# Half-array matmul pairs in the recurrence scores and the windowed attention of a two-layer encoder trunk

## The chip, the core and the metric

The kernel runs on one core of a Trainium2 chip. The metric is the device time of one execution in microseconds (us). The engines are named as in the profile: PE is TensorE (PEld its weight loads), DVE is VectorE, ACT is ScalarE, POOL is GpSimd, SP is SyncE. A core has 128 partitions; TensorE multiplies a stationary operand (up to 128 rows by 128 columns) with a moving one and writes to PSUM, which is used here as 8 banks of 512 FP32 columns.

## What is computed

Two sequences of 512 and 256 tokens, 1024 wide, go through two layers with shared weights. Each layer is a feed-forward block, a token mixer and another feed-forward block, each behind an RMS norm. The mixer of the first layer is a gated linear recurrence in both directions (8 heads of 128), that of the second a windowed attention (16 query heads in 4 groups, 64 wide, +-128 tokens, a sink logit for each head). Cut to the two mixers:

```python
# recurrence, per head and direction: S_t = diag(f_t) S_{t-1} + k_t v_t^T,  o_t = S_t^T q_t
A = einsum('bthk,btshk,bshk->bhts', qf, exp(rel), kf)   # within a chunk
o = einsum('bthk,bhkv->bthv', qf * exp(b), S) + einsum('bhts,bshv->bthv', A, vf)

# windowed attention, per block of 128 queries against up to three blocks of 128 keys
s = where(mask, einsum('bnqhgd,bnkhd->bnhgqk', q, k) * d ** -0.5, -inf)
m = maximum(max(s), sink)
p = exp(s - m); denom = sum(p) + exp(sink - m)
o = einsum('bnhgqk,bnkhd->bnqhgd', p / denom, v)
```

## The kernel before

The 768 tokens are handled together as 6 blocks of 128 (`NBLK`), 4 of the long sequence and 2 of the short. Most matrix products are made of three matmuls on a rounded FP32 type (`F32R`): an operand is split into a high half (a cast by ScalarE) and a low half (a subtraction by VectorE) by `split`, and high x high, high x low and low x high are accumulated (`mm3`, L258 to L260). The feed-forward blocks, whose matmuls are at L418 and L482, aren't touched by the change. Plain FP32 operands are used in the recurrence itself.

*Recurrence.* `hgrn` works through the 8 heads. `hgrn_scan` does one head: within each block of 128 tokens, the 128 x 128 matrix `A` of scores (rows are keys, columns are queries, both directions together) is built in 7 levels of doubling size `J` = 1 to 64, plus the diagonal. At each level ScalarE gathers the keys into `kop` (L699), `scan_scores` multiplies each block's keys with that block's queries (L674: six FP32 matmuls of 128 x 128 x 128 into two banks, 4 blocks in one and 2 in the other), and `put` writes the entries that belong to this level into `A` on VectorE: a plain copy at level 0 (L688), a masked copy (`copy_predicated`, L693) at the others. Then VectorE multiplies the decays into the queries (L716) and keys (L720) for the next level. The generator yields after each level, and `weave` puts pieces of the next head's projections (matmuls at L258 to L260) between two levels. Each engine gets its instructions in the order in which the program issues them.

*Attention.* `swa` projects keys and values (`put_kv`) and queries (`put_q`), applies the rotary embedding (`rotate`), and works through 24 units, one for each of 4 groups and 6 query blocks, each with 4 heads. A unit has stages: `query` splits its queries into halves that lie side by side, `turn` transposes them (L913), so that 64 partitions hold the high half and 64 the low half; `scores` multiplies them with the transposed keys, where the high half of the keys stands on both sets of 64 partitions, and then the low half (two matmuls a head, L1109 and L1110, so all four products); a fused VectorE instruction adds the band and takes the minimum (L1112); `exps`, `sink` and `denominator` make probabilities; `probs` transposes them (L1147) and splits them into halves; `values` multiplies them with the values, whose halves lie side by side as 128 stationary columns (L1159, L1160, 512 moving columns each); `finish` adds the two halves (L1165, L1170). `split_out` splits the outputs once more for the output projection `out_proj`. `pipeline` sorts the stages of all units by a hand-written step and rank, with pieces of the query projection and of the output projection as fillers.

Of the kernel before, what the change touches and what calls it, by code (L numbers as in the profile page):

```python
# [27 lines left out]
KV = 4  # L28
# [19 lines left out]
class Trunk:  # L48
# [621 lines left out]
    def scan_scores(self, pss, lhs, rhs):  # L670
        nc = self.nc
        for b in range(NBLK):
            s, i = (0, b) if b < 4 else (1, b - 4)
            nc.tensor.matmul(pss[s][:, i * P : (i + 1) * P], lhs(b), rhs(b), start=True, stop=True)  # L674

    def hgrn_scan(self, hd, v):
# [19 lines left out]
        for l in range(LEVELS):  # L696
            c, J = T >> l, 1 << l
            kv = bass.AP(k.tensor, k.offset, [list(k.ap[0]), [2 * J, c // 2], [T + J, 2], [1, J]])
            nc.scalar.copy(kop.rearrange("p (b g j) -> p b g j", g=2, j=J), kv)  # L699

            def rhs(b):
                return bass.AP(
                    q.tensor, q.offset + b * P, [list(q.ap[0]), [2 * J, P // (2 * J)], [T + J, 2], [1, J]]
                )

            pss = [self.ps(n) for _, n in SEQS]
            self.scan_scores(pss, lambda b: blk(kop, b), rhs)
            put(l, pss)
            if l == 0:
                pss = [self.ps(n) for _, n in SEQS]  # L710
                self.scan_scores(pss, lambda b: blk(kd, b), lambda b: blk(qs, b))
                put(LEVELS, pss)
# [12 lines left out]
            tot, base = totals, nbase  # L725
            yield
# [76 lines left out]
    def hgrn(self, lb_row, gn_row, next_row):  # L803
# [92 lines left out]
        self.drain(self.out_proj("hg_o", 0, uT, None))  # L896
        self.drain(self.out_proj("hg_o", 1, uT, next_row))

    def rotate(self, ps, heads, pos, t):
        nc = self.nc  # L900
        v = lambda t: t.rearrange("p (h d) -> p h d", d=HD)
        x, tv = v(ps), v(t)
# [12 lines left out]
    def swa(self, next_row):  # L915
# [3 lines left out]
        kT = [self.big([P, 2, T], F32R) for _ in range(KV)]  # L919
        vv = [self.big([P, 3, KV, P], F32R) for _ in range(2)]  # L920

        def put_kv(s, b, ps):
            off, n = SEQS[s]
            gb = off // P + b
            st = self.big([P, KV, 2, P], F32R)
            kh, kl = st[:, :, 0, :], st[:, :, 1, :]
            k = self.tmp(256)
            self.rotate(ps[:, :256], KV, b, k)
# [3 lines left out]
            src = ps[:, 256:].rearrange("p (g d) -> p g d", d=HD)  # L932
            v = vv[gb // 3][:, gb % 3]
            nc.scalar.copy(v[:, :, :HD], src)
            nc.vector.tensor_sub(v[:, :, HD:], src, v[:, :, :HD].bitcast(F32))

            def rest():
                for g in range(KV):
                    pt = self.ps(256)
                    for i in range(2):  # L940
                        self.transpose_r(pt[:, i * P : (i + 1) * P], st[:, g, i, :])
                    nc.scalar.copy(kT[g][:, :, gb * P : (gb + 1) * P], pt.rearrange("p (a b) -> p a b", a=2))
# [6 lines left out]
        def put_q(half):  # L949
            def f(s, b, ps):  # L950
# [4 lines left out]
                self.rotate(ps, 512 // HD, b, t)  # L955
# [6 lines left out]
        tiles = [None] * NC  # L962
        of = {}

        def units(gs):
            def alloc(g):
                if g not in of:
                    of[g] = self.big([P, 2, T])
# [8 lines left out]
        def split_out(gs):  # L977
            for g in gs:
                for i in range(2):
                    for s, (off, n) in enumerate(SEQS):  # L980
                        if s == 0:
                            tiles[2 * g + i] = self.big([P, 2, T], F32R)
                        t = tiles[2 * g + i]
                        hi, lo = t[:, 0, off : off + n], t[:, 1, off : off + n]
                        src = of[g][:, i, off : off + n]
                        nc.scalar.copy(hi, src)
                        nc.vector.tensor_sub(lo, src, hi.bitcast(F32))  # L987

        q = itertools.chain(self.proj_tok("q0", put_q(0)), self.proj_tok("q1", put_q(1)))
        wo = self.out_proj("sw_o", 0, tiles, None)  # L990
# [6 lines left out]
        extra.append((60, lambda: split_out((0,))))  # L997
        extra.append((65, lambda: split_out((1,))))
        extra += [(66 + i * 5 / 4, piece(wo)) for i in range(24)]
        extra.append((84, lambda: split_out((2,))))  # L1000
        self.pipeline(list(units(range(KV))), extra)
        split_out((3,))
        self.drain(wo)
        self.drain(self.out_proj("sw_o", 1, tiles, next_row))

    def out_proj(self, tag, half, act, next_row):
        for c in range(2):
            for b in range(NBLK):
                ps = self.ps()
                sl = slice(b * P, (b + 1) * P)  # L1010
                for i in range(4):
                    key = (tag, half, c, i // 2)
                    wh, wl = self.take(key)
                    t = act[half * 4 + i]
                    self.mm3(ps, (t[:, 0, sl], t[:, 1, sl]), (wh[:, i % 2, :], wl[:, i % 2, :]), i == 0, i == 3)
# [32 lines left out]
    def pipeline(self, units, extra):  # L1048
# [5 lines left out]
        for i, u in enumerate(units):  # L1054
            t = 4 * i
            at(t - (3 if i else 5), 5, u.query)
            at(t - 2, 3.5, u.turn)
            for h in range(GQ):
                at(t + h // 2, 0, lambda u=u, h=h: u.scores(h))
# [15 lines left out]
class Unit:  # L1075
    def __init__(self, k, s, b, g, q, kT, vv, of):
        self.k, self.s, self.b, self.g, self.q = k, s, b, g, q
        self.kT, self.vv, self.of = kT[g], vv, of
# [7 lines left out]
        self.split = {}  # L1086

    def query(self):
        k = self.k
        q = self.q().rearrange("p (h d) -> p h d", d=HD)  # L1090
        self.st = k.big([P, GQ, P], F32R)
        k.split(q, self.st[:, :, :HD], self.st[:, :, HD:])

    def turn(self):
        k, nc = self.k, self.k.nc
        pt = k.ps()
        for i in range(GQ):
            k.transpose_r(pt[:, i * P : (i + 1) * P], self.st[:, i, :])
        self.qT = k.tmp(512, F32R)
        nc.scalar.copy(self.qT, pt)  # L1100

    def scores(self, i):
        k, nc = self.k, self.k.nc
        if i == 0:
            self.sc = k.big([P, GQ, 3 * P])
            self.nm, self.den, self.sk = (k.stat(GQ) for _ in range(3))
        ps = k.ps(self.nk)
        qi = self.qT[:, i * P : (i + 1) * P]
        nc.tensor.matmul(ps, qi, self.kT[:, 0, self.keys], start=True, stop=False)  # L1109
        nc.tensor.matmul(ps, qi, self.kT[:, 1, self.keys], start=False, stop=True)  # L1110
        h = self.g * GQ + i
        nc.vector.tensor_tensor_reduce(  # L1112
            self.sc[:, i, : self.nk],
            ps,
            self.band,
            -(HD**-0.5),
            k.nsinks[:, h : h + 1],
            ALU.add,
            ALU.min,
            self.nm[:, i : i + 1],  # L1120
        )
# [21 lines left out]
    def probs(self, j):  # L1143
        k = self.k
        pt = k.ps()
        for i in range(GQ):
            k.nc.tensor.transpose(pt[:, i * P : (i + 1) * P], self.sc[:, i, j * P : (j + 1) * P], k.ident)  # L1147
        hi, lo = k.tmp(512, F32R), k.tmp(512, F32R)
        k.split(pt, hi, lo)
        self.split[j] = (hi, lo)  # L1150

    def values(self, j):
        k, nc = self.k, self.k.nc
        if j == 0:
            self.po = k.ps()
        gb = self.off // P + self.k0 + j
        v = self.vv[gb // 3][:, gb % 3, self.g, :]
        hi, lo = self.split[j]
        nc.tensor.matmul(self.po, v, hi, start=(j == 0), stop=False)  # L1159
        nc.tensor.matmul(self.po, v, lo, start=False, stop=(j == self.nkb - 1))  # L1160

    def finish(self):
        k, nc = self.k, self.k.nc
        low = k.tmp(512)
        nc.scalar.copy(low[:HD, :], self.po[HD:, :])  # L1165
        of = self.of()
        lo = self.off + self.b * P
        for par in range(2):
            r = lambda t: t.rearrange("p (c a q) -> p c a q", a=2, q=P)[:, :, par, :]
            nc.vector.tensor_add(of[par * HD : (par + 1) * HD, :, lo : lo + P], r(self.po[:HD, :]), r(low[:HD, :]))  # L1170
# [114 lines left out]
```

## Time and profile before

| | |
|---|---|
| median of 3 runs | 2833.57 us (2833.03 to 3576.69) |
| the profiled execution | 2833.56 us, of which the profile's span is 2831.8 us |
| PE, PEld, DVE, ACT, POOL busy | 2790.5, 2559.2, 2203.1, 1320.2, 307.3 us |
| recurrence scans on TensorE | 580.90 to about 958 us of the span |
| attention units | about 2105 to 2300 us of the span |

A row of a group of instructions gives the line, the engine and operation, output <- inputs by the program's names (for a matmul the moving operand, then the stationary one), the shape, how often, busy time in us and the mean duration of one in ns, and then how long the engine was idle just before them and who ended that. A matmul row also says how many rows and columns of the array are active (128*128). In a timeline a row begins with start and length in us. A row of a table of windows gives the window, its length, the busy time and count of each engine, the granted TensorE clock as a share of full speed, the share of DMA and GB/s. A row of waits names who waited for whom, the total in us, the number of times and the longest.

### The profile page before, as it was taken

The page shows a single profiled execution, that of the slowest core. Times are in us where ns is not written, and L with a number is a line of the kernel's source. Part 1 is how long each engine was busy: PE and PEld are TensorE (multiplying, and loading weights), DVE is VectorE, ACT ScalarE, POOL GpSimd, SP SyncE. Part 2 cuts the span into 40 slices and gives each one's busy share as a digit, 9 for nine tenths or more (in the row PEclk, how much of TensorE's full clock was granted, in tenths as well). Part 3 has the DMA queues.
Part 4 walks back from the last instruction along what each step waited for, and adds up shares of the span by engine and source line. Part 5 has one row for each costly group of instructions (what it writes and reads, how often), then busy time and mean ns, then how long its engine had stood idle before and what let it go on. Part 6 is the DMA issues. An engine that isn't in the chain of part 4 may idle for free.

```text
span 2831.8 us, 40534 instructions
## 1 busy us (share of the span) xinstructions
PE 2790.5 (99%) x15225; PEld 2559.2 (90%) x15225; DVE 2203.1 (78%) x3846; ACT 1320.2 (47%) x2453; POOL 307.3 (11%) x306
## 2 busy tenths in 40 slices
PE   8999999999999999999999999999999899999998
PEld 8999999889899889999999999999887779999998
DVE  7888788477577558888878887887859978878877
ACT  7444443434344336444444643444457756434443
POOL 1111111000000001111111111111100001111110
PEclk9999999999999999999999999999999999999999
DMA  5554554311111133555454355554412113555543
GB/s 157 133 126 119 124 140 122 112 45 38 43 40 38 60 97 75 140 131 122 120 121 119 82 142 129 123 122 112 144 60 75 40 43 82 142 132 121 122 113 108
DMA packets 330100, 291.37 MB, mean 103 GB/s; under 512 B 11608, under 2 KB 257840, under 8 KB 329904
## 3 DMA queue, kind: packets, MB, share of 16 engines
q1 hardware_dynamic: 294064, 212.43, 25.6%
q0 software_dynamic: 31680, 62.93, 13.3%
q10 hardware_dynamic: 4160, 13.42, 1.3%
q8 instruction: 119, 1.95, 0.3%
q14 instruction: 77, 0.63, 0.1%
HBM read 216.39 MB, written 9.44 MB: 80 GB/s over the span
## 4 chain that ended last, share of the span: by engine, by line
PE 91%; DVE 6%; ACT 2%; issue 1%; DMA 0%; DVEq 0%; ACTq 0%; SPq 0%
PE ps L418 38%; PE ps L482 20%; PE ps L259 8%; PE ps L258 8%; PE ps L260 8%; PE ps L674 3%; PE ps L768 1%; DVE w L200 1%; DVE big L264 1%; PE ps L320 1%; PE ps L1147 1%; PE ps L744 1%; DVE w L167 0%; PE ps L1109 0%; DVE big L1112 0%
## 5 line engine op out<-in xcount | busy, mean ns | idle before, releaser
L418 PE MATMUL ps<-big,w 128*128 128x384 f32 x6720 | 1173.8, 335 | 1.5 <-ACT tA L435 1.4
L418 PEld LDWEIGHTS ps<-big,w 128*128 128x128 f32 x6720 | 1165.2, 188 | 8.4 <-ACT tA L435 6.4
L199 ACT CAST w<-wr 128x512 fp32r<-128x512 f32 x600 | 416.1, 707 | 689.2 <-DVE wr L213 342.8
L200 DVE TENSOR_TENSOR w<-wr,w 128x512 fp32r<-128x512 f32 (+1 forms) x520 | 447.8, 865 | 185.8 <-ACT w L199 174.8
L482 PE MATMUL ps<-w,big 128*128 128x512 f32 x2520 | 576.6, 390 | 0.7 <-DVE x L504 0.6
L482 PEld LDWEIGHTS ps<-w,big 128*128 128x128 f32 x2520 | 472.1, 188 | 100.1 <-ACT big L263 1.5
L504 DVE SCALAR_TENSOR_TENSOR x<-ps,x 128x512 f32<-128x512 f32 x468 | 304.3, 683 | 10.8 <-PE ps L260 10.0
L141 POOL DMA_DIRECT2D s<-wr x120 | 105.3, 877 | 1821.2 <-DMA wr<-in_ffn_w_dram 649.6
L258 PE MATMUL ps<-w,big 128*128 128x512 f32 x624 | 248.9, 399 | 0.3
L260 PE MATMUL ps<-w,big 128*128 128x512 f32 x624 | 244.9, 393 | 1.8 <-DVE big L327 1.0
L259 PE MATMUL ps<-w,big 128*128 128x512 f32 x624 | 244.2, 391 | 0.0
L258 PE MATMUL ps<-big,w 128*128 128x384 f32 (+2 forms) x640 | 221.4, 347 | 2.1 <-ACT big L263 2.0
L263 ACT CAST big<-tA 128x384 fp32r<-128x384 f32 x296 | 148.0, 513 | 151.5 <-DVE tA L450 70.3
L259 PE MATMUL ps<-big,w 128*128 128x384 f32 (+2 forms) x640 | 217.5, 340 | 0.7 <-DVE big L264 0.5
L260 PE MATMUL ps<-big,w 128*128 128x384 f32 (+2 forms) x640 | 216.3, 338 | 0.0
L264 DVE TENSOR_TENSOR big<-tA,big 128x384 fp32r<-128x384 f32 x296 | 180.3, 620 | 12.9 <-ACT big L263 12.0
L167 DVE TENSOR_TENSOR w<-wr,w 128x1024 fp32r<-128x1024 f32 x92 | 111.6, 1220 | 79.3 <-ACT w L166 73.6
L166 ACT CAST w<-wr 128x1024 fp32r<-128x1024 f32 x92 | 96.6, 1052 | 118.8 <-PE ps L259 100.2
L260 PEld LDWEIGHTS ps<-w,big 128*128 128x128 f32 x624 | 117.1, 188 | 28.0 <-DVE big L987 1.7
L200 POOL TENSOR_TENSOR w<-wr,w 128x512 fp32r<-128x512 f32 x80 | 123.8, 1547 | 166.9 <-ACT w L199 146.9
L259 PEld LDWEIGHTS ps<-w,big 128*128 128x128 f32 x624 | 117.4, 188 | 22.3
L258 PEld LDWEIGHTS ps<-w,big 128*128 128x128 f32 x624 | 117.3, 188 | 22.2 <-issue 0.3
(169 smaller groups left out, 3213.3 us busy)
## 6 DMA issues: line engine op xcount, KB each, us to landing
wr<-in_ffn_w_dram SPq DMA_DIRECT2D x264, 512.0 KB, 3.9
s<-in_ffn_w_dram SPq DMA_DIRECT2D x120, 256.0 KB, 3.3
s<-wr POOLq DMA_DIRECT2D x120, 256.0 KB, 4.4
wr<-wr POOLq DMA_DIRECT2D x80, 256.0 KB, 3.7
wr<-in_hg_w_in_dram SPq DMA_DIRECT2D x40, 512.0 KB, 3.8
wr<-wr POOLq DMA_DIRECT2D x20, 512.0 KB, 4.6
spill<-x ACTq DMA_DIRECT2D x12, 512.0 KB, 2.8
x<-spill ACTq DMA_DIRECT2D x12, 512.0 KB, 3.3
```

The lines of the kernel that those rows point to most:

```text
L141: self.nc.gpsimd.dma_start(out, src, accum_op=ALU.add)
L167: self.nc.vector.tensor_sub(lo, raw, hi.bitcast(F32))
L199: nc.scalar.copy(h, src)
L200: low = (eng or nc.vector).tensor_sub(l, src, h.bitcast(F32)).ins
L258: nc.tensor.matmul(out, a[0], b[0], start=first, stop=False)
L259: nc.tensor.matmul(out, a[0], b[1], start=False, stop=False)
L260: nc.tensor.matmul(out, a[1], b[0], start=False, stop=last)
L263: self.nc.scalar.copy(hi, src)
L264: self.nc.vector.tensor_sub(lo, src, hi.bitcast(F32))
L418: self.nc.tensor.matmul(ps, a[x], b[y], start=first and k == 0 and i == 0, stop=k == 3 and i == 2, skip_group_check=True,)
L482: nc.tensor.matmul(ps, a[x], w[y], start=name == chain and kp == 0 and q == 0, stop=kp == 1 and q == 2, skip_group_check=True,)
L504: self.nc.vector.scalar_tensor_tensor(x, ps, c, x, ALU.mult, ALU.add)
```

## The change

In the recurrence only half of each block of scores is computed at a level. A call of 128 keys and 128 queries becomes two, each with 64 stationary columns (64 keys) and 64 moving columns (64 queries): the first half of the keys writes partitions 0 to 63, the second half 64 to 127, of one bank for all six blocks. At levels 0 to 5 and on the diagonal, keys meet the queries of their own half; at level 6 (`J` = 64) those of the other half. `put` then writes two pieces of 64 partitions; level 6 is now a plain copy.

In the attention, keys and queries are transposed first and split afterwards. Keys stand twice, on partitions 0 to 63 and 64 to 127 (a copy by POOL before the transpose). The queries of two heads stand one above the other; `scores` handles two heads at a time, one on the upper and one on the lower 64 rows of the array, with three matmuls each, alternating between the heads, into two banks. `probs` no longer splits: the probabilities stay FP32, and `values` uses the FP32 values as 64 stationary columns, with two heads' probabilities (256 columns) into partitions 0 to 63 and those of the other two into 64 to 127. `finish` splits the result straight into the halves that `out_proj` needs, and `split_out`, `query` and the adds are gone. In `pipeline`, `turn` takes the step that `query` had.

```diff
-    def scan_scores(self, pss, lhs, rhs):
+    def scan_scores(self, lhs, rhs):
+        ps = self.ps(NBLK * 64)
         for b in range(NBLK):
-            s, i = (0, b) if b < 4 else (1, b - 4)
-            nc.tensor.matmul(pss[s][:, i * P : (i + 1) * P], lhs(b), rhs(b), start=True, stop=True)
+            for par in range(2):
+                rows = slice(par * 64, (par + 1) * 64)
+                self.nc.tensor.matmul(ps[rows, b * 64 : (b + 1) * 64], lhs(b)[:, rows], rhs(b, par), start=True, stop=True)
+        return ps
...
-        def put(level, pss):
-            for s, (off, n) in enumerate(SEQS):
-                dst = A[:, off : off + n]
-                if level == 0:
-                    nc.vector.tensor_copy(dst, pss[s])
+        def put(level, ps):
+            for par in range(2):
+                rows = slice(par * 64, (par + 1) * 64)
+                c = 1 - par if level == LEVELS - 1 else par
+                dst = A.rearrange("p (b c j) -> p b c j", c=2, j=64)[rows, :, c, :]
+                src = ps[rows, :].rearrange("p (b j) -> p b j", j=64)
+                if level in (0, LEVELS - 1):
+                    nc.vector.tensor_copy(dst, src)
                     continue
-                nb = n // P
-                m = self.masks[:, level, :].unsqueeze(1).to_broadcast([P, nb, P])
-                r = lambda t: t.rearrange("p (b j) -> p b j", b=nb)
-                nc.vector.copy_predicated(r(dst), m, r(pss[s]))
+                m = self.masks[rows, level, c * 64 : (c + 1) * 64].unsqueeze(1).to_broadcast([64, NBLK, 64])
+                nc.vector.copy_predicated(dst, m, src)
...
-            def rhs(b):
-                return bass.AP(
-                    q.tensor, q.offset + b * P, [list(q.ap[0]), [2 * J, P // (2 * J)], [T + J, 2], [1, J]]
-                )
+            def rhs(b, par):
+                part = list(q.ap[0])
+                if J == 64:
+                    return bass.AP(q.tensor, q.offset + b * P + (0 if par else T + J), [part, [1, J]])
+                at = q.offset + b * P + par * 64
+                return bass.AP(q.tensor, at, [part, [2 * J, 64 // (2 * J)], [T + J, 2], [1, J]])
...
         def put_kv(s, b, ps):
...
-            self.split(k.rearrange("p (h d) -> p h d", d=HD), kh[:, :, :HD], kl[:, :, :HD])
-            nc.scalar.copy(kh[:, :, HD:], kh[:, :, :HD].bitcast(F32))
-            nc.scalar.copy(kl[:, :, HD:], kl[:, :, :HD].bitcast(F32))
...
+            self.rotate(ps[:, :256], KV, b, st[:, :, 0, :])
+            nc.gpsimd.tensor_copy(st[:, :, 1, :], st[:, :, 0, :])
+            nc.scalar.copy(vv[:, gb], ps[:, 256:].rearrange("p (g d) -> p g d", d=HD))
...
             def rest():
+                pt = self.ps()
                 for g in range(KV):
...
+                    nc.tensor.transpose(pt[:, g * P : (g + 1) * P], col, self.ident)
+                for i in range(KV // 2):
+                    src = pt[:, i * 2 * P : (i + 1) * 2 * P].rearrange("p (g t) -> p g t", g=2)
+                    self.split(src, *(t[:, :, gb * P : (gb + 1) * P] for t in kT[i]))
...
+    def turn(self):
...
+        for i in range(2):
+            k.nc.tensor.transpose(pt[:, i * P : (i + 1) * P], q[:, i * P : (i + 1) * P], k.ident)
+        t = k.tmp(512, F32R)
+        self.qT = t[:, :256], t[:, 256:]
+        k.split(pt, *self.qT)
...
-        nc.tensor.matmul(ps, qi, self.kT[:, 0, self.keys], start=True, stop=False)
-        nc.tensor.matmul(ps, qi, self.kT[:, 1, self.keys], start=False, stop=True)
...
+        pss = [k.ps(self.nk) for _ in range(2)]
+        for j, (x, y) in enumerate(((0, 0), (0, 1), (1, 0))):
+            for par in range(2):
+                rows = slice(par * HD, (par + 1) * HD)
+                q = self.qT[x][rows, p * P : (p + 1) * P]
+                nc.tensor.matmul(pss[par], q, self.kT[y][rows, self.keys], start=j == 0, stop=j == 2)
...
-        hi, lo = k.tmp(512, F32R), k.tmp(512, F32R)
-        k.split(pt, hi, lo)
-        self.split[j] = (hi, lo)
...
+        self.pT[j] = k.tmp(512)
+        k.nc.scalar.copy(self.pT[j], pt)
...
-        nc.tensor.matmul(self.po, v, hi, start=(j == 0), stop=False)
-        nc.tensor.matmul(self.po, v, lo, start=False, stop=(j == self.nkb - 1))
+        for par in range(2):
+            nc.tensor.matmul(
+                self.po[par * HD : (par + 1) * HD, :],
+                v,
+                self.pT[j][:, par * 256 : (par + 1) * 256],
...
     def finish(self):
...
+        self.k.split(self.po.rearrange("p (c q) -> p c q", c=2), *(t[:, :, lo : lo + P] for t in self.of()))
```

TensorE's instructions in the first head's scan, levels 0 and diagonal and what follows: before (a call of FP32 stands in one row; x4 means four in a row; `big_4938` are the queries, `big_5151` holds `kop` and `A`):

```order
L260 MATMUL ps_5125<-big_4597,w_4929 128x512
L674 MATMUL ps_5154<-big_4938,big_5151 128x128 x4
L674 MATMUL ps_5155<-big_4938,big_5151 128x128 x2
L674 MATMUL ps_5164<-big_4936 128x128 x4
L674 MATMUL ps_5165<-big_4936 128x128 x2
L258 MATMUL ps_5178<-big_4590,w_4928 128x256
```

and in the changed kernel, at the same place:

```order
L260 MATMUL ps_5125<-big_4597,w_4929 128x512
L675 MATMUL ps_5154<-big_4938,big_5151 64x64 x12
L675 MATMUL ps_5169<-big_4936 64x64 x12
L258 MATMUL ps_5188<-big_4590,w_4928 128x256
L259 MATMUL ps_5188<-big_4590,w_4928 128x256
```

Six calls of 128 x 128 into two banks became twelve of 64 x 64 into one; the matmuls around them stayed.

VectorE at the same place, before (copies into `A` at L688 and L693, decays at L716, L720 and L722, a weight split at L167):

```order
L688 COPY big_5151<-ps_5154 128x512
L688 COPY big_5151<-ps_5155 128x256
L716 TENSOR_TENSOR big_4938<-big_4938,big_4937 128x2x384
L693 COPY_PREDICATED big_5151<-big_4691,ps_5164 128x512
L693 COPY_PREDICATED big_5151<-big_4691,ps_5165 128x256
L720 TENSOR_TENSOR big_4939<-big_4939,big_5152 128x192x2 x2
L167 TENSOR_TENSOR w_5204<-wr_4932,w_5203 128x1024
```

and in the changed kernel (the same operations stand at L693, L696, L718 and L722 there):

```order
L693 COPY big_5151<-ps_5154 64x6x64 x2
L696 COPY_PREDICATED big_5151<-big_4691,ps_5169 64x6x64 x2
L718 TENSOR_TENSOR big_4938<-big_4938,big_4937 128x2x384
L722 TENSOR_TENSOR big_4939<-big_4939,big_5152 128x192x2 x2
L167 TENSOR_TENSOR w_5214<-wr_4932,w_5213 128x1024
```

The copies keep their number, two a level, now of 6 x 64 columns on 64 partitions each; the diagonal's copy stands ahead of the queries' decay.

TensorE in the second unit of the attention, before (values of one unit around scores of another; `tA` holds split probabilities as the moving operand, or transposed queries as the stationary one):

```order
L1159 MATMUL ps_18717<-tA_18647,big_17942 128x512
L1160 MATMUL ps_18717<-tA_18648,big_17942 128x512
L1109 MATMUL ps_18724<-big_17938,tA_18693 128x256
L1110 MATMUL ps_18724<-big_17938,tA_18693 128x256
L1109 MATMUL ps_18728<-big_17938,tA_18693 128x256
L1110 MATMUL ps_18728<-big_17938,tA_18693 128x256
L1159 MATMUL ps_18717<-tA_18674,big_17942 128x512
L1160 MATMUL ps_18717<-tA_18675,big_17942 128x512
```

and in the changed kernel (values at L1139, scores at L1089):

```order
L1139 MATMUL ps_18949<-tA_18889,big_18262 64x256 x2
L1089 MATMUL ps_18956<-big_18258,tA_18896 128x256
L1089 MATMUL ps_18957<-big_18258,tA_18896 128x256
L1089 MATMUL ps_18956<-big_18259,tA_18896 128x256
L1089 MATMUL ps_18957<-big_18259,tA_18896 128x256
L1089 MATMUL ps_18956<-big_18258,tA_18896 128x256
L1089 MATMUL ps_18957<-big_18258,tA_18896 128x256
L1139 MATMUL ps_18949<-tA_18917,big_18262 64x256 x2
```

Two heads' scores take six matmuls, alternating between two banks, where they took four; the values of a key block take two FP32 calls of 256 columns where they took two of 512.

More of the change, by code (lines that the diff above doesn't have):

```diff
@@ L918, in swa @@
         self.later(self.spill_x)
-        kT = [self.big([P, 2, T], F32R) for _ in range(KV)]
-        vv = [self.big([P, 3, KV, P], F32R) for _ in range(2)]
+        kT = [[self.big([P, 2, T], F32R) for _ in range(2)] for _ in range(KV // 2)]
+        vv = self.big([P, NBLK, KV, HD])
         def put_kv(s, b, ps):
@@ L967, in alloc @@
                 if g not in of:
-                    of[g] = self.big([P, 2, T])
+                    of[g] = [self.big([P, 2, T], F32R) for _ in range(2)]
                 return of[g]
@@ L1055, in pipeline @@
             t = 4 * i
[L1056 to L1059, printed above, removed]
+            at(t - (3 if i else 5), 5, u.turn)
+            for h in range(GQ // 2):
+                at(t + h, 0, lambda u=u, h=h: u.scores(h))
             at(t + 2, 2, u.sink)
@@ L1077, in __init__ @@
         self.k, self.s, self.b, self.g, self.q = k, s, b, g, q
[L1078 removed]
+        self.kT, self.vv, self.of = [t[:, g % 2] for t in kT[g // 2]], vv, of
         self.off, n = SEQS[s]
@@ L1085, in __init__ @@
         self.keys = slice(self.off + self.k0 * P, self.off + self.k1 * P)
-        self.split = {}
-    def query(self):
+        self.pT = {}
+    def turn(self):
         k = self.k
[L1090 to L1094, printed above, removed]
-        k, nc = self.k, self.k.nc
[L1096 to L1100, printed above, removed]
```

114 lines of the change are left out of this document (41 added, 73 removed).

## The prediction, made before the changed kernel was run

> **What bounds the kernel now.** I read the busy shares on the page first, then the chain that ended last, then the two stages that the change touches.
>
> ```profile
> PE 2790.5 (99%) x15225; PEld 2559.2 (90%) x15225; DVE 2203.1 (78%) x3846; ACT 1320.2 (47%) x2453; POOL 307.3 (11%) x306
> ...
> PE 91%; DVE 6%; ACT 2%; issue 1%; DMA 0%; DVEq 0%; ACTq 0%; SPq 0%
> ```
>
> TensorE is the bound: 99% busy, 91% of the chain. What it no longer has to stream shortens the kernel, and work taken from VectorE or ScalarE counts only where TensorE waits for them. The stages, by a table of windows (one head of the recurrence, two short levels and one long level of it, then most of the attention), show where that is:
>
> ```profile
> core 0: us, PE busy (x) PEld busy (x) DVE busy (x) ACT busy (x) POOL busy (x), PEclk, DMA share, GB/s
> 621.90:664.50 42.60, 42.60 (x294) 39.30 (x294) 33.57 (x58) 17.46 (x32) 0.00 (x0) 1.00 0.14 38
> 632.60:636.60 4.00, 4.00 (x25) 3.54 (x24) 3.69 (x6) 0.84 (x1) 0.00 (x0) 1.00 0.45 126
> 636.60:640.70 4.10, 4.10 (x31) 3.82 (x30) 3.48 (x8) 1.44 (x2) 0.00 (x0) 1.00 0.02 5
> 645.00:650.00 5.00, 5.00 (x30) 4.36 (x29) 5.00 (x9) 1.68 (x2) 0.00 (x0) 1.00 0.38 105
> 2105.00:2300.00 195.00, 178.96 (x990) 147.18 (x989) 177.52 (x563) 142.48 (x378) 0.00 (x0) 0.99 0.16 49
> ```
>
> In the recurrence TensorE never pauses (42.60 of 42.60 us), yet VectorE is close behind: 3.48 of 4.10 us in a short level, all 5.00 in the long one. In the attention TensorE pauses 16 us and VectorE is busy 177.52 of 195 us, so there both set the pace. The granted clock is 1.00 or 0.99 throughout.
>
> **Part 1, level scores of the recurrence.** Before, 8 heads have 8 sets of scores of 6 blocks, 384 calls; the trace counts 672 + 96 = 768 matmuls at L674, so an FP32 call is two passes of 128 columns. The first row is one head's share, from a window of L674 alone; the others are a timeline around one level.
>
> ```profile
> 665.00:708.00 43.00, 12.60 (x96) 12.33 (x96) 1.00 0.13 38
> ```
>
> ```profile
> 636.17 0.39 PE L259 MATMUL ps<-big,w 128*128 128x512 f32 x1
> 636.40 0.39 PE L260 MATMUL ps<-big,w 128*128 128x512 f32 x1
> 636.63 1.50 PE L674 MATMUL ps<-big,big 128*128 128x128 f32 x12
> 637.88 0.48 PE L258 MATMUL ps<-big,w 128*128 128x512 f32 x1
> 638.20 0.40 PE L259 MATMUL ps<-big,w 128*128 128x512 f32 x1
> ...
> 624.85 2.16 PE L674 MATMUL ps<-big,big 128*128 128x128 f32 x12
> 626.84 1.51 PE L674 MATMUL ps<-big 128*128 128x128 f32 x12
> ```
>
> Twelve passes hold TensorE from 636.63 to 637.88 and stretch the next matmul by 0.09 us (0.48 against 0.39): 1.34 / 12 = 0.112 us a pass. A matmul of 512 columns starts every 0.23 us but is drawn 0.39 long, so 0.16 us of each bar is a tail beside the next matmul. A head's 12.60 us is seven such runs (level 0 and the diagonal are adjacent): without seven tails 11.5 us, times 8 is **92 us**. The run at 624.85 is the 64-column level of the head before, with its two-piece moving operand: (1.99 us to the next run) / 12 = 0.166 a pass. The change reads one contiguous piece there, so that excess goes too.
>
> After, each call is two of 64 columns into the upper and lower half of one bank: 1536 passes. A pass of 64 columns costs half of 0.112, 0.056, or a little more if part of that doesn't scale; I take 0.058. Whether two passes in different column halves run side by side, no row shows, since every row on the page says 128*128. The bounds are full overlap, 768 x 0.058 = 45 us (**-47**), and none, 1536 x 0.058 = 89 us (**-3**). I take overlap: the two halves share neither weights columns nor output partitions, and nothing in the code orders them.
>
> VectorE gives some of it back. `put` has the same 768 columns in two pieces of 384 where it had 512 and 256, hence no gain there, and its first piece now waits for nearly all scores. A short level shrinks by about 0.7 us to 3.4 us, under the 3.5 to 3.7 that VectorE needs; the long one has no slack at all. With 0.2 us handed back in some 35 of the 56 levels, the recurrence gains **-40**.
>
> **Part 2, attention on TensorE.** Timeline rows of scores over 256 and 384 keys, and a run of query transposes:
>
> ```profile
> 2106.14 0.28 PE L1109 MATMUL ps<-big,tA 128*128 128x256 f32 x1
> 2106.26 0.28 PE L1110 MATMUL ps<-big,tA 128*128 128x256 f32 x1
> ...
> 2111.13 0.33 PE L1109 MATMUL ps<-big,tA 128*128 128x384 f32 x1
> 2111.30 0.34 PE L1110 MATMUL ps<-big,tA 128*128 128x384 f32 x1
> ...
> 2102.55 0.46 PE L913 MATMUL ps<-ident_r,big 128*128 128x128 f32 x4
> 2102.85 0.47 PE L258 MATMUL ps<-w,big 128*128 128x512 f32 x1
> ...
> 658.69 1.03 PE L736 MATMUL ps<-ident_r,big 128*128 128x128 f32 x8
> 659.48 0.48 PE L258 MATMUL ps<-big,w 128*128 128x512 f32 x1
> ```
>
> ```profile
> L1109 PE MATMUL ps<-big,tA 128*128 128x256 f32 x64 | 17.1, 293 | 0.3 <-ACT tA L1100 0.2
> L1109 PE MATMUL ps<-big,tA 128*128 128x384 f32 x32 | 10.9, 340 | 0.1
> L1159 PE MATMUL ps<-tA,big 128*128 128x512 f32 x56 | 24.3, 435 | 0.6 <-ACT tA L263 0.6
> L913 PE MATMUL ps<-ident_r,big 128*128 128x128 f32 x144 | 16.7, 246 | 10.3 <-DVE big L264 8.5 <-ACT tA L263 1.6
> ```
>
> Scores: 0.12 us for 256 columns, 0.17 for 384. Before, two matmuls a head: 128 x 0.12 + 64 x 0.17 = 26 us. After, three a head, two heads side by side in the upper and lower 64 rows: 96 x 0.12 + 48 x 0.17 = 20 us with full overlap (**-6**), 40 us with none (+13).
>
> Values: before 112 matmuls of 512 columns at 0.23 = 26 us. After, true FP32: 224 passes of 256 columns at 2 x 0.112 = 0.224, overlapped 25 us (**0**), one after another 50 us (+24).
>
> Transposes: 144 before (96 for queries, 48 for keys) at (0.30 + 0.08) / 4 = 0.095 us, 14 us; after 48 + 24 = 72 in FP32 at (0.79 + 0.09) / 8 = 0.11, as at L736, 8 us: **-5** with rounding. With overlap the attention's streaming falls by 11.
>
> **Part 3, the other engines in the attention.**
>
> ```profile
> L264 DVE TENSOR_TENSOR tA<-ps,tA 128x512 fp32r<-128x512 f32 x56 | 38.3, 687 | 3.0 <-ACT tA L263 2.5
> L1170 DVE TENSOR_TENSOR big<-ps,tA 64x256 f32<-64x256 f32 x48 | 19.9, 415 | 4.3 <-ACT tA L1165 3.7
> ...
> PE ps L913 <- DVE big L264: 8.5, 6, 3.6
> PE ps L1147 <- DVE big L1141: 2.1, 2, 1.8
> ```
>
> VectorE loses the low halves of the probabilities (38.3 us) and the two adds of `finish` (19.9), and gets one subtraction of 256 columns a unit instead, 24 x 0.42 = 10 us; the query's low half only moves. ScalarE loses the query casts and the copies in `finish`. So VectorE falls from 177 to about 130 us of 195, and the waits of the query transposes on it (8.5 us) mostly go. The pause could shrink by anything from 0 to 16 us; I take **-8**, about that row. Of POOL's new work (six copies of 256 columns of keys) nothing waits but the key transposes one block later, and POOL is idle there. No DMA is moved.
>
> **Part 4, the price of changing the shape of the array.** In the changed order of TensorE's instructions the shape in use (whole, column halves, row halves) changes 275 times: 112 around the 56 runs of the recurrence, 163 in the attention. The rows bound it. Below: a change from FP32 to the rounded type at 637.88 costs only the 0.09 us that I charged to the run, so 0 beyond it. Above: if the array had to empty, the tail of 0.16 us would be exposed each time, 44 us. The nearest row is the stretch of the first matmul behind a run, 0.08 to 0.09, where a weight load shows. I take 0.08 each: **+22**.
>
> The Trainium skill, TensorEngine Tiling (Array Packing), section Key Properties, speaks against the change here: switching the tiling mode, not just the tile, drains TensorE. No row of this trace shows a switch of tiling mode; by that rule the upper end, +44, would stand in place of +22.
>
> **Sum.** -40 - 11 - 8 + 22 = -37. The profiled execution took 2833.56 us beside its span of 2831.8, the same as the median of 2833.57, so 2833.6 - 37 = **2796 us**.
>
> **The rivals.** *Switches are free* (for: 637.88; against: only the data type changes there): -40 - 11 - 8 = -59, **2774**.
>
> *The array empties at every switch*: -59 + 44 = -15, **2818**. For: the tail is there in every row. Against: nothing in the trace.
>
> *Streams overlap but weight loads go one by one.* Loads of a transposing run and of the two matmuls behind it, from the loads' timeline:
>
> ```profile
> 2102.32 0.55 PEld L913 LDWEIGHTS ps<-ident_r,big 128*128 128x128 f32 x4
> 2102.81 0.19 PEld L258 LDWEIGHTS ps<-w,big 128*128 128x128 f32 x1
> 2102.92 0.19 PEld L259 LDWEIGHTS ps<-w,big 128*128 128x128 f32 x1
> ```
>
> A full load holds the loader for 0.11 us (2102.81 to 2102.92). If halves don't load side by side, 1536 loads of 64 columns at 0.055 are 84 us (-8), 288 loads of queries at 0.11 are 32 us (+6), the values lose about 2 by starting staggered; with -5, -8 and +22: +9, **2843**. For: no two loads in the trace lie closer than such a load. Against: they all use the whole array.
>
> The Trainium skill, TensorE: Matmul & The Clock Gate, section The mechanism in Part 3, says that a weight load overlaps running matmuls only if its row group differs; column halves share theirs, row halves don't. By it the recurrence would be nearer -8 and the scores nearer -6. The trace's loads overlap running matmuls with all 128 rows in both (PE and PEld are busy together for 39.30 us of a head), so it doesn't hold as stated for whole-array loads.
>
> *Nothing overlaps*, the one that ends slower: -3 + 13 + 24 - 5 - 8 + 22 = +43, **2877**. Its place is the attention, where row halves need three matmuls instead of two and FP32 values twice the passes. It decides as soon as pairs save less than about half of what full overlap would.
>
> **How the numbers follow.** The forecast gets 0.38, free switches 0.17, emptying 0.15, loads one by one 0.14, no overlap 0.12, anything else 0.04. 2796 is the likeliest. The low end is the free case with no loss to VectorE and most of the pause gone (-47 - 11 - 14, about 2760), the high end the no-overlap case; beyond 2758 to 2880 I leave about 0.12. A change of 2% (57 us) is about what a measurement tells from none: under 2777 lie half of the free case and a little more, 0.13; over 2890 no overlap with emptying, 0.06; the rest, 0.81, is within.
>
> **What would show it.** Right: L675 has 192 passes a head in about 6.5 us of busy time with starts of upper and lower halves close together; short levels near 3.6 us with VectorE nearly full; scores pairs in about three strides of 0.12; TensorE's pause under 10 us between the keys' projection and the end of the attention. Wrong: passes at L675 evenly 0.055 apart, values at 0.22 each in single file, or gaps of 0.1 us and more where the shape changes.

## The result, and the profile after

| | median us | runs | against before [95%] |
|---|---|---|---|
| before, beside it | 2833.57 | 2833.03 to 2838.2, and one of 3576.69 | |
| changed kernel | **2799.71** | 2799.1 to 2800.3 | **0.9876 [0.9856, 0.9895]** |

The run of 3576.69 us lies far outside the others and is in no comparison, nor in the median above. By the medians of before (2833.57 us here, 2832.67 and 2832.82 beside the later experiments) the change saves 33 to 34 us. The forecast was 2796.

The busy shares and the engines of the chain, from the page of the changed kernel:

```profile
PE 2768.5 (99%) x16129; PEld 2493.3 (89%) x16129; DVE 2168.3 (78%) x3750; ACT 1283.9 (46%) x2383; POOL 308.6 (11%) x312
...
PE 94%; DVE 4%; ACT 1%; issue 0%; DMA 0%; DVEq 0%; SPq 0%; ACTq 0%
```

TensorE is still the bound, with 904 instructions more than before and 22.0 us less busy time. The rest of the gain is pause that closed. The windows of the changed kernel, laid on about the same places as those of before: a head of the recurrence, a short level, a long level, most of the attention.

```profile
619.70:659.20 39.50, 39.50 (x389) 34.20 (x388) 35.21 (x59) 17.26 (x33) 0.00 (x0) 1.00 0.14 41
633.70:637.50 3.80, 3.80 (x43) 3.21 (x42) 3.60 (x7) 2.17 (x3) 0.00 (x0) 1.00 0.02 4
637.50:642.70 5.20, 5.20 (x45) 4.12 (x44) 5.11 (x9) 1.00 (x2) 0.00 (x0) 1.00 0.34 101
2079.00:2266.00 187.00, 185.31 (x1145) 124.14 (x1143) 131.77 (x470) 116.58 (x341) 0.00 (x0) 1.00 0.15 48
```

A head takes 39.50 us where it took 42.60. In the attention TensorE pauses 1.7 of 187 us where it paused 16 of 195, and VectorE fell to 131.77 us. The granted clock is 1.00 in all rows (1.00 and 0.99 before). Note what the first three rows don't say: PE is drawn as 100% busy, because a matmul's bar includes its tail, and the ends of these bars are modelled. A stretch in which no matmul can start, but the tail of the last one is still drawn, can't be read from a busy share, only from where bars start. The timeline around one short level's scores in the changed kernel, PE first and then the weight loads:

```profile
633.32 0.28 PE L259 MATMUL ps<-big,w 128*128 128x256 f32 x1
633.44 0.28 PE L260 MATMUL ps<-big,w 128*128 128x256 f32 x1
633.65 0.92 PE L675 MATMUL ps<-big,big 128*64 128x64 f32 x24
634.50 0.39 PE L258 MATMUL ps<-big,w 128*128 128x256 f32 x1
634.72 0.28 PE L259 MATMUL ps<-big,w 128*128 128x256 f32 x1
```

```profile
633.33 0.19 PEld L260 LDWEIGHTS ps<-big,w 128*128 128x128 f32 x1
633.65 0.78 PEld L675 LDWEIGHTS ps<-big,big 128*64 128x64 f32 x24
634.50 0.19 PEld L258 LDWEIGHTS ps<-big,w 128*128 128x128 f32 x1
634.61 0.19 PEld L259 LDWEIGHTS ps<-big,w 128*128 128x128 f32 x1
```

Ahead of L260 the load begins with the matmul before it (633.33 beside 633.32), so it is ready in time and the matmuls are 0.12 us apart. At both ends of the run the load begins together with its own matmul, at 633.65 and 634.50: it isn't put ahead of the change of shape. From the last whole-array start to the first that again is followed normally, 633.44 to 634.72, lie 1.28 us. Without a price for the changes it would be 0.12 + 12 x 0.058 + 0.12 = 0.94. So two changes cost 0.34 us, some 0.17 each.

The starts also show what a change consists of. First nothing begins: after 633.44 the next matmul would have started at 633.56, but the run's first load comes at 633.65, and after the run's last pass (its bar of 0.22 us ends at 634.57, so it starts at 634.35) the next start was due at 634.41 and the load comes at 634.50. That is 0.09 us each time. Then the first matmul has to wait for its own load, which within one shape lies under the matmul before: 0.10 us for a whole load (634.50 to 634.72, less the stride of 0.12) and some 0.05 for the load of a half (24 passes begin over 0.70 us, and 11 strides of 0.058 are 0.64). Together 0.33.

What is inside the run, by a window over its first 0.03 us and one over the whole of it, of L675 alone:

```profile
core 0: us, PE busy (x) PEld busy (x), PEclk, DMA share, GB/s
633.64:633.67 0.03, 0.02 (x2) 0.02 (x2) 1.00 0.00 0
633.60:634.50 0.90, 0.85 (x24) 0.78 (x24) 1.00 0.09 18
```

Two matmuls, and the weight load of each, begin within 0.03 us: the halves run side by side, loads too. In the attention, runs of scores and of values show the same pattern:

```profile
2078.97 0.39 PE L260 MATMUL ps<-w,big 128*128 128x512 f32 x1
2079.29 0.97 PE L1089 MATMUL ps<-big,tA 64*128 64x256 f32 x12
2080.19 0.50 PE L258 MATMUL ps<-w,big 128*128 128x512 f32 x1
2080.53 0.40 PE L259 MATMUL ps<-w,big 128*128 128x512 f32 x1
...
2090.14 0.40 PE L260 MATMUL ps<-w,big 128*128 128x512 f32 x1
2090.47 0.65 PE L1139 MATMUL ps<-tA,big 128*64 128x256 f32 x4
2091.05 0.50 PE L258 MATMUL ps<-w,big 128*128 128x512 f32 x1
2091.39 0.40 PE L259 MATMUL ps<-w,big 128*128 128x512 f32 x1
```

Whole-array matmuls of 512 columns are 0.23 us apart. Scores: 2078.97 to 2080.53 is 1.56 us, against 0.23 + 6 x 0.12 + 0.23 = 1.18, so 0.19 for each of two changes. Values: 1.25 us against 0.23 + 2 x 0.224 + 0.23 = 0.91, 0.17 each. Two, then, of the four rivals' mechanisms are out (loads one by one, nothing side by side), and so are free switches. A change costs about what the fourth, the array that empties at each change, said. Yet the time is close to the forecast. The experiments take that apart.

### The profile page after: what moved, and what is told of

It reads as the page before. It is cut to its first block, busy times and chain, and to the rows that moved or that the text cites. A ratio compares the mean times of both kernels' runs of the same rounds, so it can differ in the third digit from the quotient of the medians.

```text
span 2797.3 us, 42176 instructions
## 1 busy us (share of the span) xinstructions
PE 2768.5 (99%) x16129; PEld 2493.3 (89%) x16129; DVE 2168.3 (78%) x3750; ACT 1283.9 (46%) x2383; POOL 308.6 (11%) x312
## 4 chain that ended last, share of the span: by engine, by line
PE 94%; DVE 4%; ACT 1%; issue 0%; DMA 0%; DVEq 0%; SPq 0%; ACTq 0%
PE ps L418 40%; PE ps L482 20%; PE ps L258 9%; PE ps L259 8%; PE ps L260 8%; PE ps L675 2%; PE ps L1139 1%; PE ps L1089 1%; PE ps L770 1%; PE ps L1129 1%; PE ps L320 1%; PE ps L746 1%; DVE w L200 0%; DVE big L264 0%; DVE w L167 0%
## 5 line engine op out<-in xcount | busy, mean ns | idle before, releaser
L258 PE MATMUL ps<-w,big 128*128 128x512 f32 x624 | 253.0, 405 | 0.3
L260 PE MATMUL ps<-w,big 128*128 128x512 f32 x624 | 244.4, 392 | 1.0 <-DVE big L327 1.0
L259 PE MATMUL ps<-w,big 128*128 128x512 f32 x624 | 244.1, 391 | 0.0
L258 PE MATMUL ps<-big,w 128*128 128x384 f32 (+2 forms) x640 | 221.6, 348 | 2.7 <-ACT big L263 1.6
L259 PE MATMUL ps<-big,w 128*128 128x384 f32 (+2 forms) x640 | 217.0, 339 | 0.7 <-DVE big L264 0.6
L260 PE MATMUL ps<-big,w 128*128 128x384 f32 (+2 forms) x640 | 215.8, 337 | 0.0
L167 DVE TENSOR_TENSOR w<-wr,w 128x1024 fp32r<-128x1024 f32 x92 | 112.0, 1220 | 69.3 <-ACT w L166 63.5
L258 PEld LDWEIGHTS ps<-w,big 128*128 128x128 f32 x624 | 117.2, 188 | 30.1 <-issue 6.8
L260 PEld LDWEIGHTS ps<-w,big 128*128 128x128 f32 x624 | 117.1, 188 | 27.1 <-DVE big L327 1.7
L259 PEld LDWEIGHTS ps<-w,big 128*128 128x128 f32 x624 | 117.4, 188 | 21.5 <-issue 0.4
```

The lines of the kernel that those rows point to most:

```text
L167: self.nc.vector.tensor_sub(lo, raw, hi.bitcast(F32))
L258: nc.tensor.matmul(out, a[0], b[0], start=first, stop=False)
L259: nc.tensor.matmul(out, a[0], b[1], start=False, stop=False)
L260: nc.tensor.matmul(out, a[1], b[0], start=False, stop=last)
```

## The experiments

The theory to test, formed on this trace: pairs overlap fully, and each change of shape costs about as much as a matmul's tail (0.16 us instead of the 0.08 taken). The rivals: changes cost 0.08 or less and something else eats the gain; and for the overlap, that only neighbouring instructions overlap.

**The recurrence's part alone**: `scan_scores` and `put` as changed, the attention as before.

> The recurrence part alone on the kernel before; the attention is as before. Theory (passes overlap fully, and the array empties at each of 112 changes of shape, 0.17 us each): about -47 + 19 and a few us of waits, so -24 us against before, ratio 0.991. Rival (a change of shape costs 0.08 us as forecast, and the recurrence alone gives the -40 of the forecast less nothing): -38 us, ratio 0.987, and then the attention part would have to cost a few us.

Measured: 2809.08 us (2807.91 to 2811.98) against 2832.67, 0.9919 [0.9905, 0.9934]: **-23.6**, the -24 of the theory and not the -38 of the rival.

**The attention's part alone**: the reverse.

> The attention part alone; the recurrence is as before. Theory (streams overlap, 163 changes of shape at 0.17 to 0.20 us take back nearly all that streaming and the removed waits bring): -9 us against before, ratio 0.997, and this and the recurrence alone add up to the whole change. Rival (a change of shape costs 0.08 us): -20 us or more. Other rival (the attention part costs time): slower by a few us.

Measured: 2822.41 us (2821.0 to 2823.11), 0.9964 [0.995, 0.9979]: **-10.3**, close to the theory's -9 and far from the rival's -20. The two parts add to -33.9, the whole change, so they can be judged apart.

**The price of a change, by itself.** Two kernels, both the changed one with 56 more transposes of the identity, one in each set of scores but level 0. In the first it stands in the middle of the run, so that the array goes to whole and back once more (112 more changes); in the second behind the run, where the array goes to whole anyway.

```diff
+        full = self.ps()
+        ps = full[:, : NBLK * 64]
         for b in range(NBLK):
+            if extra and b == 3:            # the first kernel: inside the run
+                self.nc.tensor.transpose(full[:, 384:512], self.ident, self.ident)
...
+        if extra:                           # the second kernel: behind the loop
+            self.nc.tensor.transpose(full[:, 384:512], self.ident, self.ident)
```

> The changed kernel with 56 extra whole-array transposes of the identity, one in the middle of each run of level scores, into columns of the bank that nothing reads: 112 more changes of shape. To be read against the next kernel, which has the same 56 transposes behind the runs. Theory (the array empties): 112 x 0.17 to 0.20 = 19 to 22 us slower than the next kernel, about 2826 us. Rival (only a weight load shows): 112 x 0.08 = 9 us. Rival (a change of shape is free): under 2 us.

> The changed kernel with the same 56 extra transposes, each at the end of a run, next to whole-array matmuls, so no change of shape is added. Every theory: 56 x 0.11 = 6 us slower than the changed kernel, about 2806 us.

Measured: 2819.45 us (2819.26 to 2819.94), 0.9955 [0.994, 0.9969], with the transpose inside; 2801.99 (2801.29 to 2804.11), 0.9894 [0.9879, 0.9909], behind. Same work, same loads, 112 changes apart: 17.5 us, **0.156 us a change** (0.135 to 0.167 by the ends of the runs). That is a little under the 0.17 to 0.20 of the theory, and twice the rival's 0.08. The 56 transposes alone cost 2.3 us against the changed kernel, where 6 were expected. The timeline of each, inside first (the scores are L678 in both, the transpose of the identity L675 and L680):

```profile
627.86 0.39 PE L260 MATMUL ps<-big,w 128*128 128x512 f32 x1
628.17 0.59 PE L678 MATMUL ps<-big,big 128*64 128x64 f32 x12
628.70 0.33 PE L675 MATMUL ps<-ident_r 128*128 128x128 f32 x1
628.96 0.58 PE L678 MATMUL ps<-big,big 128*64 128x64 f32 x12
629.47 0.50 PE L258 MATMUL ps<-big,w 128*128 128x512 f32 x1
629.80 0.39 PE L259 MATMUL ps<-big,w 128*128 128x512 f32 x1
```

```profile
629.89 0.39 PE L260 MATMUL ps<-big,w 128*128 128x512 f32 x1
630.21 0.92 PE L678 MATMUL ps<-big,big 128*64 128x64 f32 x24
631.06 0.33 PE L680 MATMUL ps<-ident_r 128*128 128x128 f32 x1
631.14 0.48 PE L258 MATMUL ps<-big,w 128*128 128x512 f32 x1
631.46 0.40 PE L259 MATMUL ps<-big,w 128*128 128x512 f32 x1
```

From L260 to L259 it is 1.94 us with the transpose inside and 1.57 behind, 0.37 for two changes. That is more than 2 x 0.156; in part because with the transpose inside TensorE idles 1.4 us less ahead of the scores (2.2 us in all against 3.6, by the rows of L678), so that some of the price falls into waits that were there anyway. Behind the run L258 starts 0.08 us after the transpose (631.06 to 631.14): within one shape a matmul doesn't wait for the tail before it.

**Does the order of the halves matter?** The scores' two loops swapped: three matmuls of one half, then three of the other, where they alternated.

```diff
-        for j, (x, y) in enumerate(((0, 0), (0, 1), (1, 0))):
-            for par in range(2):
+        for par in range(2):
+            for j, (x, y) in enumerate(((0, 0), (0, 1), (1, 0))):
```

> The changed kernel with the two loops of the attention's scores swapped: three matmuls of the upper half of the rows, then three of the lower, where the change alternates. Theory (two halves overlap only if they stand next to each other in TensorE's queue): up to two of three pairs are lost, 96 heads' strides of 0.12 to 0.17 us come back in part: 8 to 13 us slower than the changed kernel, 2808 to 2813 us. Rival (the queue takes a later matmul of the free half ahead): within 2 us of the changed kernel.

Measured: 2799.22 us (2798.75 to 2800.88), 0.9881 [0.9868, 0.9895]: no change. The windows of its L1089 alone, at the start of a run and over it, and its group beside the changed kernel's:

```profile
2078.02:2078.07 0.05, 0.04 (x2) 0.04 (x2) 1.00 0.00 0
2078.02:2078.95 0.93, 0.92 (x12) 0.77 (x12) 1.00 0.00 0
```

```profile
L1089 PE MATMUL ps<-big,tA 64*128 64x256 f32 x192 | 19.7, 310 | 0.0
```

```profile
L1089 PE MATMUL ps<-big,tA 64*128 64x256 f32 x192 | 19.6, 310 | 0.0
```

Two matmuls begin within 0.05 us although the second half's first one is the fourth in the program. The trace doesn't name the half of a matmul; but matmuls of 256 columns that follow each other on the same rows start 0.12 us apart, so the two must be of different halves. Each half takes its next matmul as it comes free, past those that wait for the other half. That only neighbours overlap is refuted.

**Fewer changes.** If a change costs 0.15 us, the number of runs is what to cut. Both pairs of a unit's scores at one step, and all its values at the last of their steps: 205 changes instead of 275, the same instructions.

```diff
-                at(t + h, 0, lambda u=u, h=h: u.scores(h))
+                at(t, 0, lambda u=u, h=h: u.scores(h))
...
-                at(t + 7 + j, 4, lambda u=u, j=j: u.values(j))
+                at(t + 6 + u.nkb, 4, lambda u=u, j=j: u.values(j))
```

> The changed kernel with a unit's two score pairs at one step of the attention's pipeline and all its key blocks' values at one step: 205 changes of shape where there were 275. Theory (0.16 us each, as measured by the pair of kernels with extra transposes): 11 us faster than the changed kernel, about 2789 us, less any new waits. Rival (new waits for VectorE and ScalarE take it back): no gain or slower.

Measured: **2789.45 us** (2788.31 to 2791.43), 0.9847 [0.9834, 0.9861], the fastest version here; 9.8 us below the kernel with the swapped loops, which ran on the same chip and takes what the changed one takes: 70 changes at 0.140. Of the 11 us expected, 9.8 came. The window of its attention and its values' group, and behind them the same group of the changed kernel:

```profile
2079.00:2255.00 176.00, 173.27 (x1143) 127.44 (x1140) 130.90 (x470) 116.24 (x342) 0.00 (x0) 1.00 0.16 53
...
L1139 PE MATMUL ps<-tA,big 128*64 128x256 f32 x224 | 29.7, 390 | 0.2 <-ACT tA L1131 0.2
```

```profile
L1139 PE MATMUL ps<-tA,big 128*64 128x256 f32 x224 | 36.3, 404 | 0.3 <-ACT tA L1131 0.3
```

1143 matmuls take 176 us where the changed kernel has 1145 in 187 (its window of the result). The 224 values' matmuls cover 29.7 us instead of 36.3, though their number and shape are the same: there are fewer runs, each with a tail at its end.

**The same, with values beside scores.** Values and `finish` placed directly ahead of the scores of the unit two later (200 changes).

```diff
-                at(t + 7 + j, 4, lambda u=u, j=j: u.values(j))
-            at(t + 6 + u.nkb, 4, u.finish)
+                at(t + 8, -1, lambda u=u, j=j: u.values(j))
+            at(t + 8, -0.5, u.finish)
```

> As the kernel before this one, but a unit's values and finish stand directly ahead of the scores of the unit two later: 200 changes of shape. Theory: 12 us faster than the changed kernel, about 2788 us. Rival: the values now come a step earlier for units of three key blocks and TensorE waits for their probabilities: less gain than the kernel before this one.

Measured: 2791.57 us (2789.82 to 2793.46), 0.9853 [0.984, 0.9867]. It gains most of it (-7.7 against the kernel with the swapped loops), not more: 5 changes fewer than the grouped version (0.8 us) brought nothing, and the two intervals overlap. The rival named more waiting, and there is some: TensorE waits 3.6 us between 2040 and 2280 us where the grouped kernel waits 2.7, of it 0.7 against 0.2 for probabilities (`ps L1139 <- ACT tA L1131`). With overlapping intervals it can't be said more exactly.

## Why the prediction came out, step by step

The time was forecast to 4 us, but by a sum in which errors cancel.

*The bound and the overlap held.* The 24 passes of a run begin over 0.70 us, two every 0.058, as taken. The groups of the changed kernel's recurrence:

```profile
L675 PE MATMUL ps<-big,big 128*64 128x64 f32 x1344 | 54.3, 231 | 4.2 <-ACT big L702 3.1 <-ACT big L657 0.7 <-DVE big L718 0.2
L675 PE MATMUL ps<-big 128*64 128x64 f32 x192 | 7.0, 222 | 0.0
```

It is 1536 passes, 192 a head as said, and 61.3 us of bars, 7.7 a head where 6.5 was said. The Trainium skill, TensorE: Matmul & The Clock Gate, section The mechanism in Part 3, lists that a weight load overlaps running matmuls only when its row group differs, which the column halves' don't (the text above that list also lets a load go ahead into a background weight buffer). Here the loads of both halves begin within 0.03 us (633.64 to 633.67), and the loads behind them lie beside running matmuls, 24 loads and 24 matmuls in 0.92 us. By that rule, the prediction said, the recurrence's streaming would have gained nearer 8 us; alone, with its changes of shape paid, the part gained 23.6. The loads' rival had less for it than the prediction thought: in the trace of before two loads of L1147 lie between 2209.00 and 2209.20, where one takes 0.14, so loads closer than 0.11 us were there to see.

*One row was read as another level.* Part 1 took the run at 624.85 for the 64-column level with two pieces. The diagonal stands directly behind it (626.84), so it is level 0, whose moving operand alternates between two places with every column. The change doesn't make that contiguous, and the excess doesn't all go:

```profile
619.65 1.22 PE L675 MATMUL ps<-big,big 128*64 128x64 f32 x24
620.70 0.87 PE L675 MATMUL ps<-big 128*64 128x64 f32 x24
621.50 0.39 PE L258 MATMUL ps<-big,w 128*128 128x256 f32 x1
```

Level 0 holds TensorE from 619.65 to 620.70, 1.05 us, where the run at 633.65 needs 0.70 + 0.058 = 0.75. So of the excess before, (1.99 - 1.34) x 8 = 5.2 us, 0.3 x 8 = 2.4 stay, and the -47 of full overlap was in truth about -45.

*The price of a change was the term mis-sized.* Part 4 took 0.08 from the nearest row, the stretch of the first matmul behind a run; it is 0.156, so 275 changes cost 43 us and not 22. Its upper bound (the tail exposed, 44) had the right size. The row chosen shows neither half of the price, since at 637.88 only the data type changes. The loads there, in the trace of before:

```profile
637.86 0.19 PEld L258 LDWEIGHTS ps<-big,w 128*128 128x128 f32 x1
637.97 0.19 PEld L259 LDWEIGHTS ps<-big,w 128*128 128x128 f32 x1
```

L258's load begins with the last pass of the run (636.63 + 11 x 0.112 = 637.86), one matmul ahead, and the matmul behind L258 starts at 638.20, just a pass and a matmul of 512 columns after that (637.86 + 0.112 + 0.23). Nothing is lost: the longer bar is drawn from an earlier start. That 0.08 lies near the load's part of the price (0.05 and 0.10 by the starts) is luck; the 0.09 us in which nothing begins is what the forecast left out. Key Properties in the Trainium skill, TensorEngine Tiling (Array Packing), said that switching the mode drains TensorE. The traces fit that, with 0.156 us for a switch. But the next load begins 0.07 us before the drawn end of the last bar (634.50 against 634.57), and that end is modelled: whether the 0.09 us is the array emptying or something else about the change isn't shown.

*VectorE's give-back was too large, or not put to the test.* 7 us were charged, and TensorE's idle time ahead of L675 is 4.2 in all (the row above), 0.2 of it ended by VectorE, where 1.7 stood ahead of L674 before. But the short levels did not shrink to 3.4 us as Part 1 had it. Two changes of shape hold them at 3.8, above the 3.60 us that VectorE needs there. In the long level it is nearly full (5.11 of 5.20). For the recurrence: -47 of streaming, +2.4 that stay at level 0, +17.5 for 112 changes and +2.5 of idle time make -24.6; measured by itself it is -23.6, and by the starts of the last and first feed-forward matmuls around the stage 608.3 us became 584.9, -23.4. Part 1 with its share of Part 4 (-40 + 9 = -31) promised too much.

*The attention's pause was the other one.* Part 3 took 8 of 16 us; by the windows 14 went. All waits of PE between 2060 and 2280 us in the changed kernel:

```profile
PE ps L1074 <- DVE big L912: 1.0, 1, 1.0
PE ps L1074 <- DVE x L912: 0.4, 1, 0.4
PE ps L1139 <- ACT tA L1131: 0.3, 1, 0.3
```

The wait of the query transposes on VectorE (8.5 us before) went as said but for the 1.4 at L1074, and the smaller ones too, since VectorE is idle for 55 us of that window. But idle time is not all that a wait costs. From each matmul's start to the next one's, summed over the attention stage (last matmul of the feed-forward block before it to the first of the one behind it) of both traces:

| us from start to next start | before | after | at the change's strides, without changes of shape |
|---|---|---|---|
| scores | 27.8 | 29.0 | 19.7 |
| values | 35.1 | 34.0 | 25.1 |
| transposes | 46.4 | 43.6 | 41.8 |
| the other matmuls | 232.7 | 227.3 | 223.0 |
| sum | 342.1 | 334.0 | 309.6 |

The last column is worked out: 0.12 and 0.17 us a pair of scores, 0.224 a pair of values, and for the other two the strides of a transpose and of a matmul of 512 columns, 0.112 and 0.23, at the 16 and 45 places where another shape follows. The difference to the column after is 24.4 us for 163 changes, 0.150 each, which agrees with the 0.156 and 0.140 measured by the pairs of kernels. And before, the values stood 35.1 us where Part 2 counted 26. Of the 112, 73 were followed at 0.23, 26 at about 0.3, mostly first matmuls behind transposes, whose bars begin early as at 637.88, and 13 only after 0.38 to 2.26 us. Those 13 hold 7.0 us beyond their strides, but the idle column of the instructions behind them has only 4.2 of it: the first part of every wait lies under the tail of the bar before. Part 2's "values 0" was thus -10 (some 2 of it belong to the transposes' strides), its scores -8 and not -6, its transposes -4.6 where it had -5 (its own figures, 13.7 and 7.9, give -5.8), and what the other matmuls lost in pause -9.7. With +24.4 that is the stage's -8.1.

Hence the sum: changes of shape cost some 20 us more than forecast and level 0 kept 2.4; VectorE's give-back was 4.5 less, and streams and waits of the attention, which the idle column shows only in part, returned some 13 more (values 10, scores 2, the rest 1). That the total lay within 4 us of the measurement is partly luck: the recurrence was forecast at -31 with its changes and came at -23.4, the attention at -6 (-11 - 8 + 13) and came at -8.1. The profiled executions lie 34.5 us apart, of which these two stages are 31.5; the other 3 lie in stages that the change doesn't touch, and are within what two executions of one kernel differ by (2807.91 to 2811.98 above).

## What to carry to other kernels

Two matmuls in different halves of the array ran side by side almost fully, weight loads included (a pair of 64 columns every 0.058 us), so a pair costs what one does; but each change of the array's shape cost about 0.15 us. About 0.09 of it is time in which nothing starts, the rest a weight load that no matmul covers. Count the runs of one shape, not the matmuls: here 275 changes took back 43 of some 78 us, and two lines that put runs of one shape together returned 10. Look for it, and for short waits, in the time from start to start: bars with tails show both as work.

## What was not expected of the hardware

Each half of the array goes ahead on its own: with the loops swapped, the other half's first matmul still began within 0.05 us of the run's first (two in the window 2078.02 to 2078.07), past two that stood before it in the program. And a load that crosses a change of shape isn't issued early: it began with its own matmul at 633.65 and 634.50, while within a shape it begins one matmul ahead.
